# Products of ones on row halves, column halves and the whole array ahead of a decoder trunk

## Chip, core and metric

The kernel runs on one core of one Trainium2 chip. The metric is the device time of one execution in microseconds (us). The core has a matrix engine (TensorE, PE in the profile, with its weight loads listed as PEld), a vector engine (VectorE, DVE), a scalar engine (ScalarE, ACT), GpSimd (POOL), and queues that issue transfers (SyncE, SP, for most of them). Tiles have 128 partitions. PE multiplies a stationary tile (the weights) by a moving tile and writes to PSUM, eight banks of 512 fp32 columns per partition.

## What is computed

A decoder trunk of two layers on one sequence of 512 tokens with 1024 features, all in float32. Each layer wraps a mixer in two half-step SwiGLU blocks with 2816 hidden features; layer 0 has a chunked gated linear attention, layer 1 a stick-breaking attention.

```python
for i in range(DEPTH):
    x = x + 0.5 * swiglu(rmsnorm(x, ffn1_norm[i]), ffn1_w_gate[i], ffn1_w_up[i], ffn1_w_down[i])
    h = rmsnorm(x, mix_norm[i])
    y = gla_mixer(h, ...) if i % 2 == 0 else sb_mixer(h, ...)
    x = x + y
    x = x + 0.5 * swiglu(rmsnorm(x, ffn2_norm[i]), ffn2_w_gate[i], ffn2_w_up[i], ffn2_w_down[i])
return rmsnorm(x, final_norm)
```

The products of ones that the change adds are no part of this; their results are read by nobody.

## The kernel before

The activations are kept transposed, features on partitions: eight tiles of 128 x 512. Every fp32 operand of a large product is cut into a high and a low part in the type float32r, and a product is three matrix products: high by high, low by high, high by low (`mm3`, through `mm` at L64; the variant for seven-product blocks is at L558). Weights arrive from memory through SP's queue as `raw` tiles (L89); ACT writes the high part `wh` (L124) and DVE the low part `wl` (L126), in entries that a feed works off in order, a few entries ahead of PE.

The head of the kernel, which is where the change goes, is this. DVE clears a small tile `gl`, four transfers on ACT's queue fill it with the gains of all norms, and PE transposes it into `ps_g` (L1290); DVE copies it to `gT` (L1291), of which column 50 holds ones. SP brings in x as eight tiles `x0` with the first four weight tiles between them and behind them. PE transposes x into eight PSUM tiles `ps_x`, four products each (L1297). For each of them ACT writes the high part `xh`, scaled by the gain (L1302), and DVE the low part `xl` (L1303); ACT and DVE also copy the plain x (L1311, L1313). ACT squares x for the norm (L1320), DVE makes the reciprocal root of the sums, scales the identity by it (`dg`, L427), and PE spreads it over the partitions with products by ones (`ps_R`, L431). The first weight products (`ps_f`) start as soon as the first `xh`, `wh` and `wl` are there. After the head come, phase by phase, the SwiGLU block, the linear attention, the SwiGLU blocks around the layer boundary, the stick-breaking attention and the last block.

Within an engine the instructions stand in one queue and run in its order. The tile framework chooses the order from the program by its own planning, and puts the waits in. PSUM tiles are dealt in turn from four groups of banks, `a` (2), `z` (3), `t` (2) and `o` (1); a request without a group takes the next of the fixed order `aazzztto`.

Not all products use the whole array. In the stick-breaking attention the value products (`values`, L1155) write 64 output columns each, in turn to the lower and the upper half of the PSUM partitions; in the linear attention one level of the scores has 64 columns (`ps_S<-e`, L64). The profile lists the form of a product as rows*columns of the array in use (128*64), then the moving operand.

Of the kernel before, what the change touches and what calls it, by code (L numbers as in the profile page):

```python
# [11 lines left out]
F32R = mybir.dt.float32r  # L12
# [6 lines left out]
P = 128  # L19
# [5 lines left out]
EPS = 1e-6  # L25
LEVELS = (64, 32, 16, 8, 4, 2, 1)
NEG = -1.0e30

NEAR, NEAR_MOVING = 16, 48

# [2 lines left out]
def decoder(ctx: ExitStack, tc: tile.TileContext, a: dict, out: bass.AP):  # L33
    nc = tc.nc
# [12 lines left out]
    def psum(name, tag=None):  # L47
        if tag is None:
            tag = order[turn_[0] % 8]
            turn_[0] += 1  # L50
        return pp.tile([P, T], F32, tag=tag, bufs=banks[tag], name=name)
# [7 lines left out]
    ones = gT[:, 50:51].to_broadcast([P, P])  # L59
# [1210 lines left out]
    with tc.tile_pool(name="ip", bufs=1) as ip:  # L1270
        gl = ip.tile([P, P], F32, name="gl")
        nc.vector.memset(gl, 0.0)
        row = 0
        for nm in ("ffn1_norm", "mix_norm", "ffn2_norm"):
            nc.scalar.dma_start(gl[row : row + 16], a[nm].rearrange("l (k p) -> (l k) p", p=P))
            row += 16
        nc.scalar.dma_start(gl[row : row + 2], a["gla_o_norm"].rearrange("l (k p) -> (l k) p", p=P))
        x0 = {}
        st["ss"] = None
        sums = [ip.tile([P, NT], F32, name=f"sums{hf}") for hf in range(2)]  # L1280
        lead = phases[0].lead
        for hf in range(2):
            for i in range(NT):
                x0[i, hf] = ip.tile([P, T], F32, name=f"x0_{i}_{hf}")
                nc.sync.dma_start(x0[i, hf], a["x"][0, i * P : (i + 1) * P, hf * T : (hf + 1) * T])
            for c in lead[:1] if hf == 0 else lead[1:]:
                c.pool = ip
                c.load()
        ps = psum("ps_g")
        nc.tensor.transpose(ps[:, 0:P], gl, ident)  # L1290
        st["gains"] = nc.vector.tensor_copy(gT[:, 0:50], ps[:, 0:50]).ins  # L1291
        st["nh"], st["nl"], pst = [], [], []
        for hf in range(2):
            for k in range(hf * 4, hf * 4 + 4):
                ps = psum("ps_x")
                for i in range(NT):
                    nc.tensor.transpose(  # L1297
                        ps[:, i * P : (i + 1) * P], x0[i, hf][:, (k % 4) * P : (k % 4 + 1) * P], ident
                    )
                h = np_.tile([P, T], F32R, tag="xh", name="xh")  # L1300
                l = np_.tile([P, T], F32R, tag="xl", name="xl")
                nc.scalar.activation(h, ps, AF.Copy, scale=gT[:, k : k + 1])  # L1302
                nc.vector.scalar_tensor_tensor(  # L1303
                    out=l, in0=ps, scalar=gT[:, k : k + 1], in1=h.bitcast(F32), op0=ALU.mult, op1=ALU.subtract
                )
                st["nh"].append(h)
                st["nl"].append(l)
                pst.append(ps)
            for k in range(hf * 4, hf * 4 + 4):
                if k % 2:  # L1310
                    nc.vector.tensor_copy(xs[k], pst[k])  # L1311
                else:
                    nc.scalar.copy(xs[k], pst[k])  # L1313
        for e in feed.q[:2]:
            e.split()
        for hf in range(2):
            for i in range(NT):
                junk = ip.tile([P, T], F32, tag="j", bufs=2, name="junk")
                with tc.issue_after(st["cut"]) if hf * NT + i >= 6 else ExitStack():
                    nc.scalar.activation(junk, x0[i, hf], AF.Square, accum_out=sums[hf][:, i : i + 1])  # L1320
        st["sums"] = sp.tile([P, NT], F32, tag="rq", bufs=2, name="sums")
        nc.vector.tensor_tensor(out=st["sums"], in0=sums[0], in1=sums[1], op=ALU.add)
# [16 lines left out]
def _constants():  # L1339
# [6 lines left out]
        "c_lvl": np.concatenate(lv, axis=1).astype(np.float32),  # L1346
        "c_neg": np.where(t >= s, NEG, 0.0).astype(np.float32),
    }
# [20 lines left out]
```

## Time and profile before

| | us |
|---|---|
| median of 2 runs | 1865.07 (1864.43 to 1865.71) |
| profiled execution, its own time | 1867.25 |
| its span, first to last instruction | 1865.3 |
| PE busy | 1845.7 (99%) |
| DVE busy | 1409.8 (76%) |
| ACT busy | 1009.2 (54%) |

A row of the timeline gives the start, the duration, the engine, the line of the source, the operation, output<-inputs, the form, and how many equal instructions in succession the row merges; a bracket gives idle time ahead of it and what ended it. The duration of a product runs from its start to its modelled end and reaches over the start of the next one, so that durations of products in succession add up to more than the time they take. In the page's chain, each instruction is followed back to what released it.

### The profile page before, as it was taken

The page shows a single profiled execution, that of the slowest core. Times are in us where ns is not written, and L with a number is a line of the kernel's source. Part 1 is how long each engine was busy: PE and PEld are TensorE (multiplying, and loading weights), DVE is VectorE, ACT ScalarE, POOL GpSimd, SP SyncE. Part 2 cuts the span into 40 slices and gives each one's busy share as a digit, 9 for nine tenths or more (in the row PEclk, how much of TensorE's full clock was granted, in tenths as well). Part 3 has the DMA queues.
Part 4 walks back from the last instruction along what each step waited for, and adds up shares of the span by engine and source line. Part 5 has one row for each costly group of instructions (what it writes and reads, how often), then busy time and mean ns, then how long its engine had stood idle before and what let it go on. Part 6 is the DMA issues. An engine that isn't in the chain of part 4 may idle for free.

```text
span 1865.3 us, 29157 instructions
## 1 busy us (share of the span) xinstructions
PE 1845.7 (99%) x11945; PEld 1650.8 (88%) x11945; DVE 1409.8 (76%) x2171; ACT 1009.2 (54%) x1708; POOL 7.3 (0%) x17
## 2 busy tenths in 40 slices
PE   8999999999999999999999999999999999999998
PEld 6999999789888899999889999998888788999997
DVE  7987776675767987777788777676878669877775
ACT  6545445444555554544564445445888745554454
POOL 0000000000000000000000000000000000000000
PEclk9999999999999999999999999999999999999999
DMA  5343333211223233332243333233221222333321
GB/s 159 113 131 107 102 113 111 80 52 62 66 70 112 78 105 116 110 115 80 84 131 102 103 108 108 80 93 100 68 69 57 69 90 91 125 102 102 118 87 68
DMA packets 177513, 179.04 MB, mean 96 GB/s; under 512 B 4034, under 2 KB 167924, under 8 KB 177380
## 3 DMA queue, kind: packets, MB, share of 16 engines
q1 hardware_dynamic: 176768, 176.18, 29.7%
q8 instruction: 93, 1.52, 0.3%
q0 software_dynamic: 512, 0.99, 0.2%
q14 instruction: 40, 0.33, 0.1%
q10 hardware_dynamic: 100, 0.03, 0.0%
HBM read 175.11 MB, written 2.10 MB: 95 GB/s over the span
## 4 chain that ended last, share of the span: by engine, by line
PE 95%; DVE 2%; DMA 1%; ACT 1%; issue 0%; ACTq 0%; DVEq 0%; SPq 0%
PE ps_d L64 25%; PE ps_w L558 21%; PE ps_f L64 18%; PE ps_q L558 10%; PE ps_z L558 5%; PE ps_t L64 5%; PE ps_b L64 4%; PE ps_S L64 1%; PE ps_z L1093 1%; PE ps_bt L64 1%; PE ps_oT L1155 1%; PE ps_T L1140 1%; PE ps_o L64 1%; DMA raw<-in_ffn_w_up_dram 1%; DVE wl L126 0%; PE ps_R L431 0%
## 5 line engine op out<-in xcount | busy, mean ns | idle before, releaser
L126 DVE TENSOR_TENSOR wl<-raw,wh 128x1024 fp32r<-128x1024 f32 (+1 forms) x244 | 259.2, 1064 | 92.2 <-ACT wh L124 63.1
L124 ACT CAST wh<-raw 128x1024 fp32r<-128x1024 f32 (+1 forms) x244 | 224.8, 923 | 142.2 <-PE ps_f L64 44.3
L64 PE MATMUL ps_d<-hh,wl 128*128 128x512 f32 x672 | 262.1, 390 | 0.0
L64 PE MATMUL ps_d<-hh,wh 128*128 128x512 f32 x672 | 262.1, 390 | 0.0
L64 PE MATMUL ps_d<-hl,wh 128*128 128x512 f32 x672 | 261.4, 389 | 0.0
L558 PE MATMUL ps_w<-th,wh 128*128 128x256 f32 x864 | 238.9, 276 | 1.0 <-ACT u L600 1.0
L558 PE MATMUL ps_w<-tl,wh 128*128 128x256 f32 x864 | 238.6, 276 | 0.0
L558 PE MATMUL ps_w<-th,wl 128*128 128x256 f32 x864 | 238.6, 276 | 0.0
L124 ACT CAST wh<-s 128x1024 fp32r<-128x1024 f32 x144 | 151.1, 1049 | 121.9 <-PE ps_q L558 36.8
L126 DVE TENSOR_TENSOR wl<-s,wh 128x1024 fp32r<-128x1024 f32 x144 | 175.8, 1222 | 52.4 <-ACT wh L124 26.4
L318 DVE SCALAR_TENSOR_TENSOR x<-ps_d,x 128x512 f32<-128x512 f32 x184 | 124.7, 687 | 102.4 <-PE ps_d L64 101.8
L124 ACT CAST wh<-rawd 128x1024 fp32r<-128x1024 f32 x84 | 88.5, 1054 | 180.5 <-PE ps_d L64 98.1
L64 PE MATMUL ps_f<-xh,wh 128*128 128x512 f32 x448 | 181.5, 405 | 2.1 <-DVE q L756 1.5
L64 PE MATMUL ps_f<-xl,wh 128*128 128x512 f32 x448 | 175.1, 391 | 0.0
L64 PE MATMUL ps_f<-xh,wl 128*128 128x512 f32 x448 | 174.4, 389 | 0.0
L558 PEld LDWEIGHTS ps_w<-th,wh 128*128 128x128 f32 x864 | 162.2, 188 | 1.5 <-ACT u L600 1.4
L558 PEld LDWEIGHTS ps_w<-tl,wh 128*128 128x128 f32 x864 | 162.2, 188 | 0.0
L558 PEld LDWEIGHTS ps_w<-th,wl 128*128 128x128 f32 x864 | 162.2, 188 | 0.0
L64 PEld LDWEIGHTS ps_d<-hl,wh 128*128 128x128 f32 x672 | 126.2, 188 | 26.7
L64 PEld LDWEIGHTS ps_d<-hh,wh 128*128 128x128 f32 x672 | 126.1, 188 | 24.8
L64 PEld LDWEIGHTS ps_d<-hh,wl 128*128 128x128 f32 x672 | 126.1, 188 | 24.1
L126 DVE TENSOR_TENSOR wl<-rawd,wh 128x1024 fp32r<-128x1024 f32 x84 | 102.8, 1224 | 51.6 <-ACT wh L124 38.1
(253 smaller groups left out, 4431.8 us busy)
## 6 DMA issues: line engine op xcount, KB each, us to landing
raw<-in_ffn_w_gate_dram SPq DMA_DIRECT2D x43, 1024.0 KB, 5.4
raw<-in_ffn_w_up_dram SPq DMA_DIRECT2D x43, 1024.0 KB, 5.4
rawd<-in_ffn_w_down_dram SPq DMA_DIRECT2D x84, 512.0 KB, 3.5
raw<-in_gla_w_in_dram SPq DMA_DIRECT2D x12, 1024.0 KB, 5.5
raw<-in_sb_w_in_dram SPq DMA_DIRECT2D x16, 512.0 KB, 3.8
raw<-in_gla_w_out_dram SPq DMA_DIRECT2D x4, 1024.0 KB, 5.0
raw<-in_sb_w_in_dram SPq DMA_DIRECT2D x4, 1024.0 KB, 5.1
raw<-in_sb_w_out_dram SPq DMA_DIRECT2D x4, 1024.0 KB, 5.0
```

Of the source, the lines that this page charges most:

```text
L64: st["pe"] = nc.tensor.matmul(ps, l, r, start=first, stop=last).ins
L124: st["cut"] = nc.scalar.copy(h, r).ins
L126: nc.vector.tensor_tensor(out=l, in0=r, in1=h.bitcast(F32), op=ALU.subtract)
L318: nc.vector.scalar_tensor_tensor(out=xs[k], in0=ps, scalar=0.5, in1=xs[k], op0=ALU.mult, op1=ALU.add)
L558: st["pe"] = nc.tensor.matmul(o, l_, r_, start=first and j + n == 0, stop=j == 3 and n == 2, skip_group_check=True).ins
L1093: nc.tensor.matmul(o_, l_, r_, start=first, stop=last, skip_group_check=True)
L1140: nc.tensor.transpose(ps[:, c0 : c0 + P], ys[yb][:, yc + j * P : yc + (j + 1) * P], ident)
L1155: nc.tensor.matmul(po[e * 64 : e * 64 + 64, j * P : T], self.v[j][:, c : c + 64], self.wt[p, e][bk][:, c0 : c0 + n], start=j == 0, stop=j ...
```

## The change

A tile `one2` of 128 x 2048 float32r is filled with ones by 16 DVE copies. Three PSUM tiles are taken from group `z`. Then PE runs twelve entries of `SEQS`, each behind eight products on the whole array with 512 moving rows, with 16 more of these at the very start. An entry has a kind, a number of moving rows n, a shift d in bytes of the weights' place within `one2`, and a count:

- `row`: products on 64 of the 128 array rows, in turn on the lower half into one PSUM bank and on the upper half into another;
- `row0`: the lower row half alone;
- `col0`: 64 of the 128 array columns alone;
- `mixrow`: two products on the whole array into a third bank, then one on each row half, and so on.

All products have a start and a stop flag, so none adds to an earlier one. Their operands are slices of `one2` only. Everything else is as before; the framework orders the whole program anew, so that on DVE the square sums, the root and `dg` now stand ahead of the copy of the gains, and on ACT the squares and the high parts of the first four weight tiles stand ahead of the first `xh`.

```diff
+BASE = 0
+SEQS = (
+    ("row", 512, 0, 24),
+    ("row0", 512, 0, 12),
+    ("row", 384, 0, 24),
+    ("row", 256, 0, 24),
+    ("row", 256, 64, 24),
+    ("col0", 512, 0, 12),
+    ("row", 128, 0, 24),
+    ("row", 512, 64, 24),
+    ("col0", 512, 64, 12),
+    ("col0", 256, 0, 12),
+    ("mixrow", 512, 0, 24),
+    ("mixrow", 256, 0, 24),
+)
...
+        one2 = ip.tile([P, 2048], F32R, name="one2")
+        for i in range(0, 2048, 128):
+            nc.vector.tensor_copy(one2[:, i : i + P], ones)
+        off = (-BASE) % 256 // 4
+        pss = [psum("ps_p", "z") for _ in range(3)]
+
+        def one(o, n, d, rows=slice(0, P), cols=P):
+            t = off + (4096 + d) // 4
+            nc.tensor.matmul(
+                o, one2[rows, t : t + cols], one2[rows, off : off + n], start=True, stop=True, skip_group_check=True
+            )
+
+        lo, hi = slice(0, 64), slice(64, P)
+
+        def seq(kind, n, d, count):
+            for c in range(count):
+                if kind == "full":
+                    one(pss[0][:, 0:n], n, d)
+                elif kind == "row":
+                    one(pss[c % 2][:, 0:n], n, d, (lo, hi)[c % 2])
+                elif kind == "row0":
+                    one(pss[0][:, 0:n], n, d, lo)
...
+                elif kind == "col0":
+                    one(pss[0][lo, 0:n], n, d, cols=64)
...
+                elif kind == "mixrow":
+                    if c % 4 < 2:
+                        one(pss[2][:, 0:512], 512, 0)
+                    else:
+                        one(pss[c % 2][:, 0:n], n, d, (lo, hi)[c % 2])
...
+        seq("full", 512, 0, 16)
+        for kind, n, d, count in SEQS:
+            seq("full", 512, 0, 8)
+            seq(kind, n, d, count)
         ps = psum("ps_g")
         nc.tensor.transpose(ps[:, 0:P], gl, ident)
```

More of the change, by code (lines that the diff above doesn't have):

```diff
@@ L1288, in decoder @@
                 c.load()
+        one2 = ip.tile([P, 2048], F32R, name="one2")
[17 more added lines that the diff above has]
+                    one(pss[0][:, 0:n], n, d, lo)
+                elif kind == "col":
+                    one(pss[0][(lo, hi)[c % 2], 0:n], n, d, cols=64)
+                elif kind == "col2":
+                    one(pss[c % 2][(lo, hi)[c % 2], 0:n], n, d, cols=64)
+                elif kind == "col0":
+                    one(pss[0][lo, 0:n], n, d, cols=64)
+                elif kind == "four":
+                    r, k = c % 2, c // 2 % 2
+                    one(pss[r][(lo, hi)[k], 0:n], n, d, (lo, hi)[r], 64)
+                elif kind == "mixrow":
[3 more added lines that the diff above has]
+                        one(pss[c % 2][:, 0:n], n, d, (lo, hi)[c % 2])
+                elif kind == "mixcol":
+                    if c % 4 < 2:
+                        one(pss[2][:, 0:512], 512, 0)
+                    else:
+                        one(pss[0][(lo, hi)[c % 2], 0:n], n, d, cols=64)
+        seq("full", 512, 0, 16)
+        for kind, n, d, count in SEQS:
+            seq("full", 512, 0, 8)
+            seq(kind, n, d, count)
         ps = psum("ps_g")
```

## The prediction

> **What bounds the kernel now.** I read the page first: the span, the busy line of TensorE (PE), and the shares of the chain of work that ended last.
>
> ```profile
> span 1865.3 us, 29157 instructions
> PE 1845.7 (99%) x11945; PEld 1650.8 (88%) x11945; DVE 1409.8 (76%) x2171; ACT 1009.2 (54%) x1708; POOL 7.3 (0%) x17
> ...
> PE 95%; DVE 2%; DMA 1%; ACT 1%; issue 0%; ACTq 0%; DVEq 0%; SPq 0%
> ```
>
> PE is busy 99% of the span and holds 95% of the chain. Whatever is put into its queue adds its own time, unless it lands where PE idles. So I next read the timeline of PE over the first 28 us, the one place with idle time worth naming.
>
> ```profile
> 5.62 0.44 PE L1290 MATMUL ps_g<-ident,gl 128*128 128x128 f32 x1 [5.62 <-DMA gl<-in_ffn_norm_dram]
> 5.86 3.73 PE L1297 MATMUL ps_x<-ident,x 128*128 128x128 f32 x16
> ...
> 12.03 2.88 PE L1297 MATMUL ps_x<-ident,x 128*128 128x128 f32 x13 [0.27 <-DMA x<-in_x_dram]
> 14.66 0.47 PE L64 MATMUL ps_f<-xh,wh 128*128 128x512 f32 x1
> 14.98 0.39 PE L64 MATMUL ps_f<-xh,wl 128*128 128x512 f32 x1
> ...
> 17.95 0.39 PE L64 MATMUL ps_f<-xl,wh 128*128 128x512 f32 x1
> 18.97 0.73 PE L64 MATMUL ps_f<-xh,wh 128*128 128x512 f32 x2 [0.64 <-ACT wh L124]
> ...
> 26.62 1.12 PE L431 MATMUL ps_R<-dg,gT 128*128 128x128 f32 x8
> 27.49 0.47 PE L64 MATMUL ps_f<-xh,wh 128*128 128x512 f32 x1
> ```
>
> PE waits 5.62 us for the gains, then transposes x as it lands, and starts the first weight product at 14.66. After that it stalls once, 0.64 us at 18.97. A product's listed length (0.39) overlaps its neighbour's; its price is the interval from start to start. I take prices from stretches where nothing waits.
>
> **Prices of full products.** Three stretches of the PE timeline:
>
> ```profile
> 65.47 0.39 PE L64 MATMUL ps_d<-hl,wh 128*128 128x512 f32 x1
> ...
> 70.91 0.39 PE L64 MATMUL ps_d<-hl,wh 128*128 128x512 f32 x1
> 71.14 0.28 PE L558 MATMUL ps_w<-nh,w 128*128 128x256 f32 x1
> ...
> 73.86 0.28 PE L558 MATMUL ps_w<-th,wh 128*128 128x256 f32 x1
> ```
> ```profile
> 1334.89 0.34 PE L1093 MATMUL ps_z<-kl,mq 128*128 128x384 f32 x1
> 1335.07 0.23 PE L1093 MATMUL ps_z<-negm,idb 128*128 128x128 bf16 x1
> ```
> ```profile
> 1833.09 3.22 PE L1227 MATMUL ps_T<-ident,x 128*128 128x128 f32 x28
> 1836.06 0.47 PE L64 MATMUL ps_bt<-wh,hh 128*128 128x512 f32 x1
> ```
>
> From 65.47 to 70.91 lie 24 intervals: 5.44/24 = **0.227 us** for 512 moving rows. From 71.14 to 73.86 lie 24 more: 2.72/24 = **0.113** for 256. For 384 it is 0.18. A transpose late in the kernel takes (1836.06 - 1833.09)/28 = 0.106; early, from 12.03, (14.66 - 12.03)/13 = 0.202. So PE starts at about half speed, though the granted-clock column says 1.00 there.
>
> **Change, part by part.** It removes nothing. It adds 16 VectorE (DVE) copies, and 352 products ahead of the first transpose in PE's queue. The instruction order of the changed kernel has all 352. Counted from SEQS: 16 + 12 x 8 = 112 full ones plus 24 full ones in the two mixed runs, 136; 36 on a column half; 12 on the low row half alone; 168 alternating between row halves. Nobody reads the results, so no eviction is added.
>
> *Start.* The first product waits for nine of the copies (the ninth holds its weights). DVE is free after this memset, and a 128x128 operation costs 0.88/4 = 0.22:
>
> ```profile
> 0.87 0.17 DVE L1272 MEMSET gl<- 128x128 f32 x1
> ...
> 26.17 0.88 DVE L427 TENSOR_SCALAR dg<-ident,r 128x128 f32<-128x128 f32 x4
> ```
>
> 1.04 + 9 x 0.22 = 3.0 us. The other copies run beside PE.
>
> *Slow start.* Work from 5.62 to 9.59 left PE at half speed, and by 14.98 it was at full: half speed lasts over 4.0 and under 9.4 us of work. I take 4.6 us, near the lower end because the added run has no pauses; half is lost: 2.3 (bounds 2.0 to 4.7).
>
> *Full products:* 136 x 0.227 = 30.9. *Column halves alone:* 24 x 0.227 + 12 x 0.113 = 6.8. *Row half alone:* 12 x 0.227 = 2.7, priced as full since it streams as many moving rows. The entries that place the weights 64 bytes further I price alike; if the two placements differ by 0.01 us, 60 products move 0.6.
>
> *Alternating row halves.* No product of the kernel before uses a row half. The nearest rows are the products of L1155 on alternating column halves, against fp32 products on all columns:
>
> ```profile
> 371.23 2.74 PE L64 MATMUL ps_z<-w,ga 65*128 65x512 f32 x6
> 373.40 0.80 PE L64 MATMUL ps_f<-xh,wh 128*128 128x512 f32 x1
> 374.04 0.40 PE L64 MATMUL ps_f<-xh,wl 128*128 128x512 f32 x1
> ...
> 1332.30 2.38 PE L1155 MATMUL ps_oT<-wt,w 128*64 128x512 f32 x16
> 1334.61 0.44 PE L1093 MATMUL ps_z<-kh,mq 128*128 128x384 f32 x1
> ```
>
> Six fp32 instructions of 512 rows end where the next product begins streaming, 0.227 before 374.04: 2.58/6 = 0.43 each. The 16 of L1155 stream 4 x (512 + 384 + 256 + 128) = 5120 rows, ten times 512: one after the other 4.3 us, but they took 2.31. Something runs two at a time there, so I take row halves as overlapping in pairs. A pair still needs two weight loads. What one costs when it is not hidden shows where the tile shape changes:
>
> ```profile
> 392.38 0.39 PE L64 MATMUL ps_f<-xl,wh 128*128 128x512 f32 x1
> 392.70 0.68 PE L64 MATMUL ps_S<-e 128*64 128x64 f32 x8
> 393.31 0.50 PE L64 MATMUL ps_f<-xh,wh 128*128 128x512 f32 x1
> 393.64 0.39 PE L64 MATMUL ps_f<-xh,wl 128*128 128x512 f32 x1
> ```
>
> 393.31 to 393.64 is 0.33, 0.10 more than 0.227; I take 0.108 for a load (its own product is listed 0.50 long instead of 0.39), so a pair takes the larger of its stream and 0.216. Thirty pairs of 512: 6.8; 12 of 384, 30 of 256 and 12 of 128, each 0.216: 11.7. Together **18.5**. Bounds: no overlap, 60 x 0.227 + 24 x 0.18 + 60 x 0.113 + 24 x 0.108 = 27.3; overlap with loads side by side too, half of that, 13.7. The value taken keeps the loads one behind another, as every row here has them.
>
> The Trainium skill, "TensorE: Matmul & The Clock Gate", Part 3, says that products on different row groups run concurrently, and their weight loads too (four groups of 32 rows: 3.07 times as fast); by it the sum would be near the lower bound. No run shows it yet.
>
> *Changes of tile shape.* In the fence above entering costs 0.32 - 0.227 = 0.09; the eight column-half products last 0.61 where eight alone would need 8 x 0.058 = 0.47 by their 64-column loads (0.108/2 plus 0.004), 0.14 more, with the return's wait in it; then 0.10 again: 0.34 a round trip. The change makes 22: one in each of the ten plain entries, six in each mixed one (two full, two half products in turn). 22 x 0.34 = **7.5** (bounds 0, if row halves need no change, and 11).
>
> The Trainium skill, "TensorEngine Tiling (Array Packing)", Key Properties, has a change of tiling mode drain the engine. The 0.34 agrees for column tiles. By this rule a kernel with few products in halves gains nothing from them.
>
> Sum on PE: 30.9 + 6.8 + 2.7 + 18.5 + 7.5 = 66.4. The added run ends at 3.0 + 2.3 + 66.4 = 71.7 us.
>
> *What follows it.* By then x and the first weights have landed, and ScalarE (ACT) has split them. 33 transposes at 0.106 take 3.5; the first weight product starts at 75.2 instead of 14.66: +60.5. The 0.64 stall for wh goes (the splits stand ahead of ACT's waiting copies), and the first product no longer runs cold (0.1): -0.7. What is late next is DVE:
>
> ```profile
> 10.35 1.23 DVE L126 TENSOR_TENSOR wl<-raw,wh 128x1024 fp32r<-128x1024 f32 x1 [4.04 <-ACT wh L124]
> 12.16 1.41 DVE L1303 SCALAR_TENSOR_TENSOR xl<-ps_x,gT,xh 128x512 fp32r<-128x512 f32 x2 [0.59 <-ACT xh L1302]
> ```
>
> Its queue after the gains (0.7 us after the run's end) is one split 1.2, four xl at 0.7, two copies, four xl: the last ends about 8.5 us after the run, and PE, 24 products on from 3.6, wants it at 8.9. It fits by 0.4; were it late, that much is lost. The square sums, the root and the dg tiles now run during the products, which shortens DVE's queue. PSUM buffers are dealt in another rotation from here on; I price that at 0, bounds -2 and +2, since PE is busy 99%. The SP queue issues the same transfers; those past the first twelve wait for PE anyway.
>
> **Sum:** +60.5 - 0.7 = +59.8. The profiled execution took 1867.25 (span 1865.3), 2.2 above the median 1865.07; added to the median this gives **1924.9**, 3.2% slower. Two per cent (37 us) is about what a measurement of this kernel can tell from no change.
>
> **Rivals.**
> *No overlap of row halves* (the change then does not do what its alternation suggests): 27.3 instead of 18.5, 1933.7. For it: in the trace only column halves, and fp32 ones, speak for overlap. Against: 2.31 where 4.3 was due.
> *Cheap halves:* shape changes cost nothing and loads overlap: 66.4 - 7.5 - 4.8 = 54.1, 1912.6. Against: the 0.34 seen.
> *Exposed loads:* in tile mode each of 216 half products waits for its load, 216 x 0.108 = 23 more: 1948. Against: the eight of L64 run at about 0.06 each.
> *Not slower:* products that nobody waits for, with equal weights, cost only their load, 352 x 0.108 = 38.0 and no changes of shape: the run ends at 43.3, +31.4, **1896.5**, within 2%. It decides once the sum on PE falls below 43.9. Against: 24 intervals at 0.227. The rest of the kernel cannot give the difference back: PE idles under 20 us in all.
> The Trainium skill, "TensorE: Matmul & The Clock Gate", section Back-to-back issue gap, gives about 131 ns for 512 rows in a sustained stream, which points that way; the trace has 227 and disagrees.
>
> **How the numbers follow.** Forecast 0.51, no overlap 0.25, cheap halves 0.15, exposed loads 0.06, not slower 0.03. The range from 1911 to 1938 takes in the first three with 2 us for the slow start and the rotation. All but the last case are over 2% slower: slower 0.965, within 2% 0.03, faster 0.005.
>
> **What would show it.** The first weight product near 75 us; full products at 0.227 and, early, about 0.43; alternating 512s at about half the interval of the row half alone, 256s and 128s no faster than 0.108 each; a gap near 0.1 at each change of shape, in both directions. After it the timeline should run as before, shifted by 60 us. I am wrong if alternation brings nothing, if the half products are far from these prices, or if the later kernel moves by over 2 us.

## The result and the profile after

The changed kernel takes 1920.9 us (1920.69 to 1921.12, two runs) against 1865.07: a ratio of 1.0296, 95% interval 1.0275 to 1.0317. It is 55.8 us slower. The profiled executions differ by 53.4 us (1920.69 against 1867.25; spans 1918.7 against 1865.3).

The page of the changed kernel, in the rows that answer to those of before (span, busy time, shares of the chain by engine):

```profile
span 1918.7 us, 29871 instructions
PE 1904.5 (99%) x12297; PEld 1692.9 (88%) x12297; DVE 1411.1 (74%) x2187; ACT 1009.9 (53%) x1708; POOL 7.3 (0%) x17
...
PE 95%; DVE 2%; ACT 1%; DMA 1%; issue 0%; DVEq 0%; ACTq 0%; SPq 0%
```

PE has 352 more products and 58.8 us more of busy time; ACT and DVE are busy within 1.3 us of before. The timeline of PE at the end of the added run, and at the first 256-row product of the later kernel:

```profile
66.08 0.33 PE L1352 MATMUL ps_g<-ident,gl 128*128 128x128 f32 x1
...
69.84 0.50 PE L79 MATMUL ps_f<-xh,wh 128*128 128x512 f32 x1
...
125.37 0.28 PE L573 MATMUL ps_w<-nh,w 128*128 128x256 f32 x1
```

The run ends at 66.08 instead of 71.7 as forecast. The first weight product is 55.2 us later than before (69.84 against 14.66), the first 256-row product 54.2 (125.37 against 71.14), the end of the span 53.4. So the added run is the whole of the difference; the head gives back about 1 us and the later kernel another 0.8.

Inside the run, the rows of the weight loads (PEld) show the entries best, because the form of a row changes with the shape: 128*128 is a full product, 64*128 one on a row half. From the start of one row to the start of the next is the time of the first.

```profile
2.38 6.68 PEld L1313 LDWEIGHTS ps_p<-one 128*128 128x128 f32 x24 [2.38 <-DVE one L1307]
9.42 2.61 PEld L1313 LDWEIGHTS ps_p<-one 64*128 64x128 f32 x24 [0.35 <-issue]
12.38 1.68 PEld L1313 LDWEIGHTS ps_p<-one 128*128 128x128 f32 x8 [0.35 <-issue]
14.42 2.61 PEld L1313 LDWEIGHTS ps_p<-one 64*128 64x128 f32 x12 [0.35 <-issue]
17.38 1.69 PEld L1313 LDWEIGHTS ps_p<-one 128*128 128x128 f32 x8 [0.35 <-issue]
19.42 2.05 PEld L1313 LDWEIGHTS ps_p<-one 64*128 64x128 f32 x24 [0.35 <-issue]
21.72 1.69 PEld L1313 LDWEIGHTS ps_p<-one 128*128 128x128 f32 x8 [0.25 <-issue]
...
23.77 1.50 PEld L1313 LDWEIGHTS ps_p<-one 64*128 64x128 f32 x24 [0.36 <-issue]
25.39 1.68 PEld L1313 LDWEIGHTS ps_p<-one 128*128 128x128 f32 x8
...
35.66 1.41 PEld L1313 LDWEIGHTS ps_p<-one 64*128 64x128 f32 x24 [0.35 <-issue]
37.15 1.68 PEld L1313 LDWEIGHTS ps_p<-one 128*128 128x128 f32 x8
...
42.17 9.95 PEld L1313 LDWEIGHTS ps_p<-one 128*128 128x128 f32 x50 [0.36 <-issue]
52.48 0.19 PEld L1313 LDWEIGHTS ps_p<-one 64*128 64x128 f32 x2 [0.35 <-issue]
...
53.58 0.18 PEld L1313 LDWEIGHTS ps_p<-one 64*128 64x128 f32 x2 [0.37 <-issue]
```

Twenty-four products of 512 on alternating halves take 2.96 us (9.42 to 12.38), and so do twelve on the low half alone (14.42 to 17.38): the halves run in pairs. The 24 of 384 take 2.30, of 256 1.62, of 128 1.49. Eight full products behind a half entry take 2.04 where 8 x 0.227 is 1.82, so a change of shape costs 0.2 at each end of an entry. A group of the mixed entry (two half, two full) repeats every 1.10 us (52.48 to 53.58). One pair and two full products at 0.23 each make 0.69: a round trip costs 0.4. The products on 64 columns (the row of 50 from 42.17 on has them in it) show no gap, and no change of shape.

### The profile page after: what moved, and what is told of

Its sections match the earlier page's. It is cut to its first block, busy times and chain, and to the rows that moved or that the text cites. A ratio compares the mean times of both kernels' runs of the same rounds, so it can differ in the third digit from the quotient of the medians.

```text
span 1918.7 us, 29871 instructions
## 1 busy us (share of the span) xinstructions
PE 1904.5 (99%) x12297; PEld 1692.9 (88%) x12297; DVE 1411.1 (74%) x2187; ACT 1009.9 (53%) x1708; POOL 7.3 (0%) x17
## 4 chain that ended last, share of the span: by engine, by line
PE 95%; DVE 2%; ACT 1%; DMA 1%; issue 0%; DVEq 0%; ACTq 0%; SPq 0%
PE ps_d L79 24%; PE ps_w L573 20%; PE ps_f L79 17%; PE ps_q L573 10%; PE ps_z L573 5%; PE ps_t L79 4%; PE ps_b L79 3%; PE ps_p L1313 3%; PE ps_S L79 1%; PE ps_bt L79 1%; PE ps_z L1108 1%; PE ps_oT L1170 1%; PE ps_T L1155 1%; PE ps_o L79 1%; DVE wl L141 0%; DVE l L1133 0%
```

## The experiments

Each is an edit of the changed kernel, and its time is read like that of the change, against the kernel before on the same chip.

**One half alone.** Does the alternation really save time, or does the record only show starts close to each other?

```diff
-                    one(pss[c % 2][:, 0:n], n, d, (lo, hi)[c % 2])
+                    one(pss[c % 2][:, 0:n], n, d, lo)
```

> All alternating products use the low row half alone, in the same two banks, so nothing can overlap. Theory (row halves run in pairs, so that 168 products took about 13.9 us): now 60 x 0.228 + 24 x 0.172 + 60 x 0.115 + 24 x 0.111 = 27.4 us, 13.5 more, 1934.4. Rival (the 3 ns between the starts of a pair is only a record, and half products are cheap by themselves): 1920.9 as for the changed kernel.

It took 1936.45 us, 70.6 above the kernel before on the same chip (1865.83) where the change is 55.8 above: 14.8 more. The weight loads of this kernel:

```profile
9.50 5.33 PEld L1313 LDWEIGHTS ps_p<-one 64*128 64x128 f32 x24 [0.35 <-issue]
15.18 1.69 PEld L1313 LDWEIGHTS ps_p<-one 128*128 128x128 f32 x8 [0.35 <-issue]
...
81.52 0.14 PEld L1352 LDWEIGHTS ps_g<-ident,gl 128*128 128x128 f32 x1
```

And a window of it (length, then busy time and count of PE, PEld, DVE, ACT, POOL, then granted clock, share of transfers, GB/s):

```profile
46.50:49.80 3.30, 3.30 (x9) 2.19 (x8) 0.00 (x0) 0.00 (x0) 0.00 (x0) 0.50 0.00 0
```

The 24 of 512 now take 5.68 instead of 2.96, and the added run ends at 81.52 instead of 66.08. The overlap is real. Of these 15.4 us the lowered clock takes 1.7, half of a stretch of 3.4 us, so the overlap is worth 13.7 where 13.5 was expected. The rest of the median's 14.8 is probably lowered clock as well: the profiled execution (1937.61, mean clock 0.997) has a second such stretch in the later kernel (674.4 to 677.8), and the one with mean clock 0.999 took 1934.49, where 1934.4 was expected.

**Mixed entries sorted.** The same products with fewer changes of shape.

```diff
-                    if c % 4 < 2:
+                    if c < 12:
```

> The two mixed entries keep their 12 full and 12 half products but run them as two blocks, 1 round trip of tile shapes instead of 6 each. Theory (the extra of a mixed entry is 0.39 us a round trip): 10 x 0.39 = 3.9 less, 1917.0. Rival (the extra belongs to the products or to the third bank): 1920.9.

1916.76 us, 50.9 above the kernel before: 4.9 less than the change. From the row that begins the eight full products behind the shifted `row` entry of 512 (42.17 above, 43.10 here) to the end of the run:

```profile
43.10 12.22 PEld L1313 LDWEIGHTS ps_p<-one 128*128 128x128 f32 x60 [0.36 <-issue]
55.67 1.23 PEld L1313 LDWEIGHTS ps_p<-one 64*128 64x128 f32 x12 [0.35 <-issue]
...
62.93 0.14 PEld L1352 LDWEIGHTS ps_g<-ident,gl 128*128 128x128 f32 x1
```

19.83 us against 23.91: ten round trips saved 4.08, 0.41 each. The extra belongs to the change of shape. The other 0.8 of the 4.9 is not explained; the four runs lie between 1915.67 and 1919.03.

**Only the first 16 full products, or none.** Does work in PE's early idle time cost anything, and does the new order of the other engines? The edit shown is that of the second kernel; the first keeps the 16 and drops the other entries alike.

```diff
-SEQS = (
-...
-)
+SEQS = ()
...
-        seq("full", 512, 0, 16)
+        seq("full", 512, 0, 0)
```

> Only the 16 full products at the very start are left. Theory (PE idles until x has landed near 12 us, so work that ends at about 7.5 us is free): 1865 within 1.5, at best 1 us less than before since the clock is already full when the second half of x is transposed. Rival (PE is busy 99%, so its products add their time): 5.1 more, 1870.

> The 16 copies and the three PSUM tiles stay, all 352 products go. Theory (the new order of DVE and ACT and the other rotation of banks are worth under 1 us, and the 0.8 us that the later kernel regained comes from them): 1864 to 1865.5. Rival (the new order of the head costs by itself, since the square sums and the root now stand ahead of the copy of the gains on DVE): 2 to 4 more, up to 1869.

The first took 1864.99, a ratio of 0.9995 (0.9986 to 1.0004); the second 1865.38, 0.9998 (0.9989 to 1.0007), both against 1865.83. Neither can be told from no change. The weight loads of the first:

```profile
2.39 6.35 PEld L1300 LDWEIGHTS ps_p<-one 128*128 128x128 f32 x16 [2.39 <-DVE one L1294]
...
11.49 1.40 PEld L1346 LDWEIGHTS ps_x<-ident,x 128*128 128x128 f32 x13 [0.38 <-DMA x<-in_x_dram]
13.25 0.19 PEld L66 LDWEIGHTS ps_f<-xh,wh 128*128 128x128 f32 x1 [0.35 <-ACT x L1362]
```

Six microseconds of products are free: PE still waits for x at 11.49, and the first weight product starts at 13.25 instead of 14.66, since x was there 0.5 earlier in this execution and the last 13 transposes now take 0.108 each (the load row of 1.40), where before they took 0.202 (12.03 to 14.66). Nobody behind them is faster by that much, and the total moves by less than its interval. The small differences of the later kernel are not settled. From the first 256-row product to the end the profiled execution of before takes 1794.2, that of the changed kernel 1793.3 and that without products 1792.3: so the 0.8 is no work of the products, and as the profiled execution of before was 2.2 above its median, it can't be told from scatter.

**56 full products and no entries.** These end after x has landed.

```diff
+SEQS = ()
...
-        seq("full", 512, 0, 16)
+        seq("full", 512, 0, 56)
```

> 56 full products and no entries. They end near 16.9 us, after x has landed. Theory (the run shifts the transposes and the first weight product, which starts 3.7 us behind its end instead of at 14.66; the head gives 0.95 back): 5 more less up to 0.8 of the later drift, 1870. Rival 1 (all of it adds): 14.3 more, 1880. Rival 2 (only what reaches past 14.66 adds): 2.2 more, 1868.

1873.48 us, 7.9 more than before (ratio 1.0041, 1.0027 to 1.0055): more than the theory's 5 and far from both rivals. The run ended where it should (16.87). PE, then ACT of this kernel, and its windows with the granted clock (the column behind POOL):

```profile
16.98 3.66 PE L1346 MATMUL ps_x<-ident,x 128*128 128x128 f32 x32
22.65 0.56 PE L66 MATMUL ps_f<-xh,wh 128*128 128x512 f32 x1 [2.01 <-ACT x L1362]
```
```profile
17.18 1.28 ACT L413 ACT_TABLE_LOAD   x1
...
18.59 1.03 ACT L126 CAST wh<-raw 128x1024 fp32r<-128x1024 f32 x1
19.70 2.42 ACT L1351 ACTIVATE xh<-ps_x,gT 128x512 fp32r<-128x512 f32 x4
```
```profile
22.60:26.40 3.80, 3.75 (x10) 2.97 (x10) 3.80 (x7) 3.28 (x6) 0.00 (x0) 0.55 0.77 246
```

The table load, the root (left out above, 0.20) and the weight split that the new order put ahead of `xh` were hidden by the long run. Behind a short one they are not: `xh` starts 2.8 us after the run ends, and PE waits 2.0. The theory lacked this wait. And just then the clock drops to half for 3.4 us, so that the next eight products start every 0.43 instead of 0.23, some 1.7 more. But this is the slowest of the five executions (1874.74, mean clock 0.998); the other four, at 0.999, took 1.1 to 2.0 less, so the fall is probably not in them. Of the median's 7.9, the forecast 5 and the wait of 2.0 leave 0.9 open.

**Price of the weight loads.** Other entries: among them 24 products each of `full`, `row0`, `row` and `col0`, with 256 down to 32 moving rows.

```diff
+    ("full", 256, 0, 24), ("full", 256, 64, 24), ("full", 128, 0, 24), ("full", 128, 64, 24),
+    ("full", 64, 64, 24), ("row0", 256, 64, 24), ("row0", 128, 64, 24), ("row0", 64, 64, 24),
+    ("row", 128, 64, 24), ("row", 64, 64, 24), ("row", 32, 64, 24), ("col0", 128, 64, 24),
```

> Other entries, 24 products each: full 256 (weights unshifted and shifted by 64 bytes), full 128 (both), full 64, row0 256, 128 and 64, row 128, 64 and 32, col0 128; all but the first with the shift. Theory (a load of 128 float32r columns takes about 0.107 us, one load hides behind one product, and the loads of the two row halves run side by side): full and row0 of 128 and of 64 all at about 0.11 a product, row pairs of 128, 64 and 32 all at about 0.11 a pair, col0 128 at about 0.06; in all about 1914, up to 4 more if the clock falls in the thin entries. Rival (the floor is an issue cost a pair, not the load): 64 and 32 rows get cheaper, 0.06 a product, about 1906.

1918.43 us in one run; the clock did fall, for 10.2 us. Full products of 128 rows, then of 64; alternating halves of 64, with the full products behind them, then of 32, again with what follows:

```profile
20.18 2.65 PEld L1313 LDWEIGHTS ps_p<-one 128*128 128x128 f32 x23
...
29.23 2.65 PEld L1313 LDWEIGHTS ps_p<-one 128*128 128x128 f32 x23
...
56.67 1.41 PEld L1313 LDWEIGHTS ps_p<-one 64*128 64x128 f32 x24 [0.39 <-issue]
58.13 1.67 PEld L1313 LDWEIGHTS ps_p<-one 128*128 128x128 f32 x8
...
60.15 1.41 PEld L1313 LDWEIGHTS ps_p<-one 64*128 64x128 f32 x24 [0.35 <-issue]
61.59 1.86 PEld L1313 LDWEIGHTS ps_p<-one 128*128 128x128 f32 x9
```

23 loads take the same time for 128 and for 64 moving rows, and 12 pairs of 64 or of 32 take 1.46 and 1.44, 0.2 of it for the change of shape. So at 128 rows and below a float32r product costs its weight load, 0.11, and the loads of the two row halves run beside each other: 0.11 a pair, 0.055 a product. A fixed cost of starting a product would look alike, but `col0`, with 128 moving rows too and half of the weight columns, takes 0.059 a product: the cost goes with the load. That pairs too wait for their loads, and not for a fixed 0.055 a product, is argued and not shown in float32r; in bf16 (next experiment) pairs of 128 rows start 0.056 apart, 0.028 a product, so there at least no such fixed cost holds. The Trainium skill, "TensorE: Matmul & The Clock Gate", section LDWEIGHTS, has a load take its columns divided by 1.2 ns; for 128 columns that is an estimate of 107 ns. The 0.11 agrees.

**The same in bf16.** A bf16 copy of the tile, and other entries: row halves, column halves (`col` alternates them in one bank, `col2` in two) and quarters of the array (`four`).

```diff
+        oneb = ip.tile([P, 2048], BF16, name="oneb")
+        nc.vector.tensor_copy(oneb, one2.bitcast(F32))
...
-                o, one2[rows, t : t + cols], one2[rows, off : off + n], ...
+                o, oneb[rows, t : t + cols], oneb[rows, off : off + n], ...
```

> All products of the added run in bf16, entries: row 512, 256, 128; col0 512; col 512 (column halves in one bank), col2 512 (in two banks), col 128; four 512 and 128 (row half times column half); full 128; mixrow 512; mixcol 512. Theory (halves of either kind overlap, loads side by side, every change of tile shape about 0.4 us a round trip): col and col2 of 24 last as long as 12 of col0, four half of that, both mixed entries alike, full 128 at 0.06 a product; about 1917. Rival (only row halves overlap): col and col2 twice col0, mixcol 1.3 us longer than mixrow; about 1926.

1913.32 us in one run. The weight loads of `col0` (12), `col` (24), `col2` (24) and `four` (24), all 512 rows, each with the row behind it:

```profile
22.99 2.30 PEld L1315 LDWEIGHTS <-oneb 128*64 128x64 bf16 x12 [0.42 <-issue]
25.70 1.41 PEld L1315 LDWEIGHTS <-oneb 128*128 128x128 bf16 x8 [0.41 <-issue]
27.53 2.30 PEld L1315 LDWEIGHTS <-oneb 128*64 128x64 bf16 x24 [0.42 <-issue]
30.25 1.41 PEld L1315 LDWEIGHTS <-oneb 128*128 128x128 bf16 x8 [0.41 <-issue]
32.08 2.30 PEld L1315 LDWEIGHTS <-oneb 128*64 128x64 bf16 x24 [0.42 <-issue]
34.79 1.41 PEld L1315 LDWEIGHTS <-oneb 128*128 128x128 bf16 x8 [0.41 <-issue]
...
39.24 1.01 PEld L1315 LDWEIGHTS <-oneb 64*64 64x64 bf16 x24 [0.42 <-issue]
40.66 1.41 PEld L1315 LDWEIGHTS <-oneb 128*128 128x128 bf16 x8 [0.41 <-issue]
```

Twelve on one column half take 2.71; 24 on alternating column halves 2.72, in one bank or in two (2.71); 24 on four quarters 1.42. So column halves overlap as row halves do, and quarters four at a time. Eight full products behind a half entry take 1.83 (25.70 to 27.53), 0.1 above their 8 x 0.216. A group of the mixed entry repeats every 0.86, and a pair and two full products make 0.65: in bf16 a round trip costs 0.21, half of that in float32r. The second part of the theory, 0.4 for any round trip, was wrong for bf16.

**The same in fp32.** Products with the shift d = 64 are made fp32.

```diff
+            if d == 64:
+                return nc.tensor.matmul(o, one2[rows, t : t + cols].bitcast(F32), one2[rows, off : off + n].bitcast(F32), ...)
```

> Entries with the shift of 64 bytes are now fp32 (two passes a product), 8 products each: full 512, col0 512, col 512 (alternating column halves), col0 64, row 512, row0 512, full 128, row 128; then col0 512 in float32r. Theory (the two passes of an fp32 product on 64 columns run side by side on the array's two column halves, which is why 16 of L1155 took 2.31 us and why that form costs a change of shape while float32r on 64 columns does not): full 0.86 a product, col0 and col both 0.43, row pairs 0.86, row0 0.86; about 1912. Rival (products on different column halves overlap each other): col0 alone 0.86, col 0.43; about 1915.

1913.19 us in one run. The loads of eight products on one column half end with the row at 25.48, those of eight on alternating ones with 31.11:

```profile
18.47 0.19 PEld L1311 LDWEIGHTS ps_p<-one 128*64 128x64 f32 x2 [0.36 <-issue]
...
25.48 1.68 PEld L1314 LDWEIGHTS ps_p<-one 128*128 128x128 f32 x8 [0.81 <-issue]
27.52 0.20 PEld L1311 LDWEIGHTS ps_p<-one 128*64 128x64 f32 x4 [0.35 <-issue]
...
31.11 1.68 PEld L1314 LDWEIGHTS ps_p<-one 128*128 128x128 f32 x8 [0.81 <-issue]
```

7.01 us against 3.59, so the rival was right: an fp32 product (two instructions of 0.43) on 64 columns takes 0.86 alone, and two on opposite column halves overlap. That is what L1155 does in the kernel before, and why its 16 instructions took 2.31 us.

**When does the clock fall?** In e1_low and e4_load it fell at the end, or 0.4 us behind the end, of an entry of thin products (128 or 64 moving rows) on one row half, with PE busy throughout. It fell without such products too: behind PE's wait of 2.0 us in e7_56, behind one of 1.1 us in the later kernel of e1_low, and in the head of e8_none (12.6 to 15.9), where PE had waited for x. A last kernel looks at the busy case and has long entries of each kind.

```diff
+SEQS = (
+    ("row", 128, 64, 96),
+    ("full", 128, 64, 96),
+    ("row0", 512, 64, 48),
+    ("row0", 128, 64, 96),
+)
```

> Entries row 128 x 96, full 128 x 96, row0 512 x 48, row0 128 x 96. Theory (the clock falls where only half of the array's rows work and each product streams for half of its interval, as in the entries that e1_low and e4_load ran when it fell): full speed in the first three (pairs of 0.11, products of 0.11, products of 0.23), half speed for one or more stretches of 3.4 us within or just behind row0 128, whose products then take 0.21; about 1909 plus 1.7 for each stretch. Rival (thin products lower it whichever half, or the fall was chance): it falls in row 128 or full 128 too, or nowhere.

1915.95 us in one run. Windows within the four entries, the last one in two parts, and behind them (columns as above):

```profile
10.30:15.40 5.10, 5.10 (x94) 5.10 (x96) 0.00 (x0) 2.30 (x6) 0.00 (x0) 1.00 1.19 305
17.90:27.90 10.00, 10.00 (x92) 10.00 (x91) 1.72 (x9) 1.70 (x3) 0.00 (x0) 1.00 0.76 242
30.40:41.20 10.80, 10.80 (x47) 8.58 (x47) 0.00 (x0) 0.00 (x0) 0.00 (x0) 1.00 0.00 0
43.80:47.70 3.90, 3.90 (x36) 3.90 (x37) 0.00 (x0) 0.00 (x0) 0.00 (x0) 1.00 0.00 0
47.90:60.50 12.60, 12.60 (x60) 12.55 (x59) 0.00 (x0) 0.00 (x0) 0.00 (x0) 0.50 0.01 1
60.60:64.80 4.20, 4.20 (x21) 4.20 (x21) 3.28 (x5) 2.37 (x4) 0.00 (x0) 0.50 0.00 0
```

PE is busy throughout, and the clock is full in the first three. It falls in the thin products on one half, 4 us after they began: 0.11 a product before 47.8, 0.21 after, to the end of the entry. It stays low for 4 us more, while PE transposes on the whole array. One half with 512 moving rows keeps the clock, and so do the whole array and alternating halves with 128. This was seen in one execution, and the thin entry always came last; its place was not varied. In e1_low, e4_load and here the fall begins between 46.0 and 47.8 us, but the changed kernel, e2_sep, e3_bf16 and e5_fp32 run through that time at full clock, so the time alone does not make it. The Trainium skill, "TensorE: Matmul & The Clock Gate", Part 1, has idle windows lower the clock; here it fell at 100% busy time in the profile, so busy time in the profile does not tell when it will; what decides it instead stays open.

## Why the prediction was right, and where it was off

The forecast was 1924.9, the measured time 1920.9.

- **Bound.** Right: PE's added time is the difference, and e1_low moved the total by what it added to PE's run.
- **Start.** The first product started at 2.38, not 3.0 (-0.6): a copy takes 2.32/16 = 0.145 in succession, not the 0.22 of another operation.
- **Slow start.** The first 24 products took 7.04 us (2.38 to 9.42) where 24 x 0.227 and a change of shape make 5.5: 1.5 lost, not 2.3 (-0.8), and below the bound of 2.0. The early products start 0.43 apart as forecast, but only up to 5.3, some 3 us of work instead of over 4.0.
- **Full products, column halves, row half alone.** Right within 0.3 us.
- **Alternating row halves.** The overlap was the right case. The step "the value taken keeps the loads one behind another" failed: the loads of the two halves overlap too (e4_load). I priced the 54 pairs of 384, 256 and 128 at 0.216; less 0.19 a plain entry for the change of shape they measure 0.176, 0.12 and 0.11, some 4.6 us less in all. The lower bound of 13.7 was the truth (about 13.9). By the prediction's own sign, 256s and 128s no faster than 0.108 each, this step was wrong: they took 0.06 and 0.054 each.
- **Changes of shape.** 7.5 was right by two errors against each other: a round trip costs 0.40 (e2_sep 0.41), not 0.34; and there are 19, not 22, for float32r products on 64 columns make none. At each change the first product of the new shape starts 0.09 late, as forecast, and the second 0.11 late (9.42 to 9.76, 12.38 to 12.72, where 0.23 is usual), about the load of 128 columns; the rows I took the price from have a load of 64 columns at one end. They were fp32 products, and those do pay on 64 columns.
- **What follows.** The transposes and the wait behind them took 3.8, not 3.5, and the head gave back 0.9, not 0.7. DVE's queue did fit. The splits and the root came early enough only because the run was long: e7_56 shows 2 us of waiting when it isn't, and in its profiled execution some 1.7 of lowered clock.
- **Later kernel.** -0.8, within the bounds given.
- **Sum.** From the run's end -5.6, then 0 and -0.8: the span grew by 53.4, not 59.8. Adding this to the median hid 2.4 of the miss, because the profiled execution of before was 2.2 above its median and that of after 0.2 below. The 2% that the prediction gives as what a measurement can tell is too wide: the ratio of 1.0296 has an interval of 0.2% to either side.

No overlap is refuted by e1_low. Cheap halves was half right: the loads do overlap, the changes of shape are not free. Exposed loads and the price of 131 ns are refuted by the counts above: 0.23 for 512 float32r rows, 0.216 in bf16.

## What to carry to other kernels

In this kernel, work on PE was free where it ended before the operands of the next stage had landed (16 products of 512 cost nothing that could be measured); 56 of them, ending 2.2 us past the old start of the first weight product, cost 7.9, among it 2.0 of waiting for ACT, whose order of work had changed. Products that use half of the rows are worth alternating, and for short moving operands above all since their weight loads overlap as well (0.055 us a product instead of 0.11); so are products on half of the columns in bf16 and fp32 (float32r was not tried). But sort them into blocks, since each round trip between shapes costs 0.4 us in float32r and 0.2 in bf16. The price and the number of the changes of shape were taken from rows of another data type, and the sum came out right only because one was too low and the other too high: look for the row with the same type first.

## What was not expected of the hardware

- An fp32 product of 512 rows takes 0.86 us whether it uses 64 or 128 columns; alternating column halves bring it to 0.45 a product (3.59 us for eight).
- In float32r the 64-column products behave as full ones (no gap at their borders), while fp32 and bf16 ones do not.
- The clock can fall to 0.50 with PE at 100% in the profile, in or right behind thin products on one row half, and stays low in the full products that follow: 17 us in e9_thin, 4 of them behind the entry; 10.2 in e4_load, nearly all behind it; 3.4 in e1_low.
- Whether row halves may write the same bank at once was not tried.
